# Rotary score products of a latent attention: 128 rows with zeros in place of 64 rows

## The chip, the cores and the metric

The kernel runs on one core of a Trainium2 chip. The metric is the device time of one execution in microseconds (us), lower is better. The engines are named as in the profile: PE (TensorE, the matrix engine; PEld is its weight load), DVE (VectorE), ACT (ScalarE), POOL (GpSimd) and SP (SyncE, which here issues DMA transfers).

## What is computed

One layer of an encoder for two groups of 256 tokens (512 tokens in all), 1024 features, float32: a token mixer with two branches (retention, and an attention over compressed latents), a merge, and a gated convolution with a down projection. What the change touches is the score of the attention's 8 heads:

```python
def _mla_attention(q_nope, q_rope, k_nope, k_rope, v):
    ...
        s = jnp.einsum('bqhd,bkhd->bhqk', qn, k_nope) + jnp.einsum('bqhr,bkr->bhqk', qr, k_rope)
        p = jax.nn.softmax(s.astype(jnp.float32) * scale, axis=-1).astype(v.dtype)
        return jnp.einsum('bhqk,bkhe->bqhe', p, v)
```

A head's query and key have 128 features without position (nope) and 64 rotary ones (rope). The rotary key is one for all heads.

## The kernel before, in words

PE multiplies in a rounded 32-bit format (fp32r), so each float32 matrix is held as two exact parts, high and low (`_h` and `_l`; `split` makes them with a cast on ACT and a subtraction on DVE), and a product is three: high by high, high by low, low by high (`mm3`, lines 157 to 159).

**The rotary part of the scores.** For the rotary key there are two tiles of 128 partitions by 512 tokens, filled at lines 670 to 677 from one transposed bank (`ps_kr`): `K2` holds the high part twice, in partitions 0 to 63 and again in 64 to 127, and `KL` holds the low part twice in the same way. For a head's rotary query, `mla_proj` fills a tile `q2` of 128 partitions: for even heads (parity `i` = 0) the high part lies in partitions 0 to 63 and the low part in 64 to 127, for odd heads the other way round. So the product of `q2` with `K2` over all 128 partitions (line 754) gives high by high and low by high in one go. The third product, high query by low key (line 755), is taken over the 64 partitions that hold the query's high part, the slice `hp`.

`scores(h, g)` handles one head and one group of 256 tokens (a unit): for each of two query tiles of 128 it issues five products of 256 columns to a half of a PSUM bank (three of `mm3`, line 754, line 755). DVE then takes the maximum of each row (line 757), ACT the exponentials (line 761), and DVE scales by the inverse sums. There are 16 units, so line 755 is issued 32 times.

**The order.** PE's order in this part is written by hand: `mla()` issues the scores of unit n, steps of the next heads' projections (`mla_proj`: `ps_qn`, `ps_kn`, `ps_qr`, `ps_v`), the transposes of unit n - 2 (`flip`, line 775, four of 128 columns to `ps_pt`) and the weighting of unit n - 4 (`weigh`, `ps_av`). `interleave` puts products of the two branches' gates (`ps_gb`, `ps_ga`) between them. The other engines' orders are made by a scheduler when the program is built. The weights of `mla_proj` (`wm`) and of the gates (`wgb`, `wga`) arrive by DMA as raw tiles and are split on ACT and DVE beside the scores.

**Tiles.** `t512` takes a tile of 128 partitions by 512 columns from a pool of 69, which come round as they are let go; `K2` and `KL` are held until the last scores.

```python
                mm3(o, cut(qn, slice(None), qc), cut(kn, slice(None), kc), True, False)
                pe.matmul(o, q2[:, qc], K2[:, kc], start=False, stop=False)
                pe.matmul(o, q2[hp, qc], KL[hp, kc], start=False, stop=True)
```

Of the kernel before, what the change touches and what calls it, by code (L numbers as in the profile page):

```python
# [18 lines left out]
# share of other products between those of the attention, and of the last head of the retention  # L19
FILL_MLA, FILL_RET = 0.46, 7.0  # L20
# chunks of the retention branch's gate that are computed with the attention
EARLY_GA = 1
# rows of w_down, in tiles, whose products are done token tile by token tile at the end
TAIL = 12
# products that keep TensorE's clock up while it waits for the first inputs
# [21 lines left out]
def _const_table():  # L47
    """Tables that depend on the shapes alone: identity, rotary tables, decay exponents."""
    f = np.float32
    cols = {}  # L50

    def angles(dim):
        inv = (f(1.0) / (f(10000.0) ** (np.arange(0, dim, 2, dtype=f) / f(dim)))).astype(f)
        return (np.arange(S, dtype=f)[:, None] * inv[None, :]).astype(f)

    cols["ident"] = np.eye(128, dtype=f)
    ar = angles(128)
    cos, sin = np.cos(ar).astype(f).T, np.sin(ar).astype(f).T
    scale = f(128.0 ** -0.5)
    cols["cosq"] = np.concatenate([cos, cos], 0)  # L60
    cols["sinq"] = np.concatenate([-sin, sin], 0)
    cols["cosk"] = cols["cosq"] * scale
    cols["sink"] = cols["sinq"] * scale
    am = angles(64)
    cm, sm = np.cos(am).astype(f), np.sin(am).astype(f)
    cols["cosm"] = np.concatenate([cm.T, cm.T] * 2, 0)
    cols["sinm"] = np.concatenate([-sm.T, sm.T] * 2, 0)
    two = lambda a: a.reshape(2, 128, 64).transpose(1, 0, 2).reshape(128, 128)
    cols["cost"] = two(np.concatenate([cm, cm], 1))
    cols["sint"] = two(np.concatenate([-sm, sm], 1))  # L70
    p = np.arange(128)[:, None]
    j = (p // 64 * 16 + p % 16) * 16 + np.arange(16)[None, :]
    cols["expo"] = -np.abs(j - 255).astype(f)
    at, where = 0, {}
    for k, v in cols.items():
        where[k] = (at, at + v.shape[1])
        at += v.shape[1]
    return np.ascontiguousarray(np.concatenate(list(cols.values()), 1).astype(f)), where
# [11 lines left out]
def interleave(main, filler, ratio):  # L90
    """Runs main; after each step, filler for ratio times main's cost so far. Then the rest of filler."""
    spent, done = 0.0, 0.0
    alive = True
    for cost in main:
        spent += cost
        while alive and done < ratio * spent:
            try:
                done += next(filler)
            except StopIteration:
                alive = False  # L100
    drain(filler)
# [8 lines left out]
def encoder_kernel(ctx: ExitStack, tc: tile.TileContext, ins, outs):  # L110
# [96 lines left out]
    def k_cols(w, k0, k, c0, f, name, step=1024):  # L207
        """Rows k0*128.. of w (as p k f), f columns from c0."""
        h, l = w_chunk(lambda raw: [(kf(raw, k, f), w[:, k0:k0 + k, c0:c0 + f])], k * f, name, step)
        return kf(h, k, f), kf(l, k, f)  # L210

    # first loads, in the order of their use: x and the first shift and scale, then the latents' weights
# [7 lines left out]
    def load_ada(q, k):  # L220
        """256 columns of the shift and of the scale, rows k * 128.."""
        raw = ada_raw[q, k] = t512(F32, f"wada{q}_{k}")
        src = w_ada[:, k, :].rearrange("p (s f) -> p s f", f=D)[:, 0:2, q * 256:(q + 1) * 256]
        nc.sync.dma_start(halves(raw), src)
# [25 lines left out]
    # vectors by rows, turned to features on partitions later  # L250
# [30 lines left out]
    def keep_warm(n):  # L281
        """Products that nothing reads: TensorE's clock is full only while it is busy."""
        for _ in range(n):
            pe.matmul(warm, ones, wide, start=True, stop=True)
# [14 lines left out]
    def rstd_of(var, eps, n, name):  # L299
        """(var + eps) ** -0.5 for [128, n]."""  # L300
        ve, rs = small(n, name + "_ve"), small(n, name + "_rs")
        dve.tensor_scalar(out=halves(ve) if len(var.shape) == 3 else ve, in0=var, scalar1=eps, scalar2=None, op0=ALU.add)
        pool.tensor_tensor(out=rs, in0=ve, in1=half_m[:, :n], op=ALU.pow)
        return rs

    def ln_mv(parts, name):
        """Mean and variance, and rstd, of rows that lie in parts of equal length."""
        st = spool.tile([128, 12], F32, tag="st", name=name + "_st", bufs=6)
        for i, part in enumerate(parts):
            dve.bn_stats(out=st[:, 6 * i:6 * i + 6], in_=part)  # L310
        mv = small(2, name + "_mv")
        dve.bn_aggr(out=mv, in_=st[:, :6 * len(parts)])
        return mv, rstd_of(mv[:, 1:2], LN_EPS, 1, name)
# [7 lines left out]
    def norm_x():  # L321
        """Layernorm of x, rows of tokens, in place."""
# [17 lines left out]
    # vectors with features on partitions  # L340
# [17 lines left out]
    def ada_sums(q, ks=range(NK)):  # L358
        """Four rows of weights at a time, each to its own 32 columns of the array and partitions of the bank."""
        if ks[0] == 0:  # L360
            ps_ada[q] = ps512(f"ps_ada{q}")
        for k in ks:
            o = 32 * (k % 4)
            pe.matmul(ps_ada[q][o:o + 32, :], c32[:, k, :], ada_raw.pop((q, k)), start=(k < 4), stop=(k >= 4))
# [7 lines left out]
    def ada_done(q):  # L372
        """Rows to features on partitions, the sum of the four parts, the biases."""
# [13 lines left out]
    def modulated(ps_of, sc, sh, k, groups, dst, name, on_act, between=None):  # L387
        """dst = parts of ps * sc + sh for feature tile k."""
# [54 lines left out]
    dscr = dpool.tile([128, 16], F32, name="dscr")  # L443

    def decay_start():
        """Powers of sigmoid(decay), as (1 + e ** -decay) ** -distance."""
# [11 lines left out]
    def decay_tile(h):  # L458
        """Decay of key k (row) towards query 255 - m (column m)."""
        d = t512(F32, f"decay{h}")  # L460
        for kt in range(2):
            src = bass.AP(dscr.tensor, dscr.offset + h * 512 + kt * 128, [[1, 128], [1, 256]])
            nc.gpsimd.dma_start(d[:, kt * 256:(kt + 1) * 256], src)
        return d

# [5 lines left out]
    def ada_chunk(which, cc):  # L471
        """512 columns of one adaptive parameter: a generator of its steps."""
# [38 lines left out]
    # ================= start: latents of the attention =================  # L511
    with tc.manual_schedule(engines={PE}):
# [4 lines left out]
        # gate of the attention branch: kept before its sigmoid  # L517
# [33 lines left out]
        # gate of the retention branch: its first chunks are kept before the sigmoid  # L551
# [84 lines left out]
        # latents: root mean square norms, rotary key, then features on partitions  # L636
# [33 lines left out]
        K2, KL = t512(F32R, "K2"), t512(F32R, "KL")  # L670
# [5 lines left out]
        sub(KL[0:64], ps[0:64], as32(K2[0:64]))  # L676
        act.copy(KL[64:128], as32(KL[0:64]))
        take(fill_b, 2.6)

        # ================= latent attention =================  # L680
# [6 lines left out]
        def rope(ps, cos, sin, block, name):  # L687
            """Rotates the halves of each block of partitions."""
# [56 lines left out]
        def scores(h, g):  # L745
# [3 lines left out]
            hp = slice(64 * i, 64 * i + 64)  # L749
            for qt in range(2):  # L750
# [4 lines left out]
                pe.matmul(o, q2[hp, qc], KL[hp, kc], start=False, stop=True)  # L755
# [70 lines left out]
        # ================= the branch's output =================  # L826
# [16 lines left out]
        # ================= retention =================  # L843
# [109 lines left out]
        # a step of the later parameters now and then  # L953
# [15 lines left out]
        # ================= merge =================  # L969
# [32 lines left out]
        # ================= first residual and norms =================  # L1002
# [10 lines left out]
        def residual(ps, xr, gate, name):  # L1013
            """alpha * x + gate * ps, in place of x."""
# [54 lines left out]
        # ================= gated convolution =================  # L1069
# [4 lines left out]
        def up_weights(f, small_tiles=False):  # L1074
            """Parts of the weights of feature tile f: functions of (k, which half)."""
# [51 lines left out]
        # ================= down projection, second residual and norm =================  # L1127
# [6 lines left out]
        def down_w(c, k0, n, small_tiles=False):  # L1134
            """Parts of n rows of weights: a function of (row, first column, last column)."""
# [7 lines left out]
        def finish(t, c, a, b, ps):  # L1143
            """Columns a..b of half c of token tile t: residual and its sums."""
# [8 lines left out]
        for c in range(2):  # L1153
# [3 lines left out]
            # (token tile, first column, last column, bank); the last piece is small  # L1157
# [66 lines left out]
```

## Time and profile before

| what | value |
|---|---|
| time, median of 3 runs | 895.59 us (895.43 to 895.75) |
| profiled execution, first to last instruction (its span) | 893.5 us |
| profiled execution, its own device time | not shown apart from the span; the runs' median is 2.1 us above the span |
| PE busy | 877.2 us, 98% of the span, 4485 products |
| PEld busy | 736.5 us, 82% |
| DVE busy | 570.4 us, 64% |
| ACT busy | 354.3 us, 40% |
| POOL busy | 49.8 us, 6% |
| mean granted clock of PE | 0.994 of full speed |

How to read it: products on PE are pipelined, and the profile models their ends, so a product's duration is longer than the time that it takes from the next one. The start of each is recorded, and the distance from one start to the next (called a step here) tells what a product costs the sequence.

### The profile page before, as it was taken

To read this page: it belongs to the slowest core of one execution; us is meant where nothing else is said; L and a number is where in the kernel's file an instruction comes from. 1 tells how busy PE (TensorE), PEld (TensorE's weight loads), DVE (VectorE), ACT (ScalarE), POOL (GpSimd) and SP (SyncE) were. 2 spreads that over 40 slices of the span, in tenths; PEclk is the share of its full clock that TensorE was granted. 3 is DMA by queue.
4 is the path that set the end of the run, shared out by engine and by line. 5 is a ranking of instruction groups with operands and counts; after the bars stand their busy time and mean duration, and the time that the engine had idled before them with its cause. 6 is when DMAs were issued, how large, how long until landed. Compare 5 with 4: busy or idle time off the path is not lost.

```text
span 893.5 us, 11463 instructions
## 1 busy us (share of the span) xinstructions
PE 877.2 (98%) x4485; PEld 736.5 (82%) x4485; DVE 570.4 (64%) x950; ACT 354.3 (40%) x585; POOL 49.8 (6%) x78
## 2 busy tenths in 40 slices
PE   8999999999999999999998999999999999999996
PEld 5778788888889898988886899888888888888885
DVE  5475877684677777885974966447755755323456
ACT  3555766562343443353342166333333343212200
POOL 3030000000000001000020200000000000100001
PEclk9999999999999999999998999999999999999999
DMA  9922212233545425344356323234334533622401
GB/s 302 388 83 60 70 57 92 67 123 95 153 142 182 113 95 153 131 169 161 111 185 206 111 95 94 60 106 153 119 100 137 160 102 122 208 81 93 142 23 71
DMA packets 118374, 114.29 MB, mean 128 GB/s; under 512 B 6853, under 2 KB 97187, under 8 KB 118320
## 3 DMA queue, kind: packets, MB, share of 16 engines
q1 hardware_dynamic: 114688, 104.00, 35.4%
q0 software_dynamic: 2912, 8.45, 3.3%
q10 hardware_dynamic: 720, 1.11, 0.3%
q8 instruction: 35, 0.57, 0.3%
q14 instruction: 19, 0.16, 0.0%
HBM read 109.34 MB, written 4.20 MB: 127 GB/s over the span
## 4 chain that ended last, share of the span: by engine, by line
PE 94%; DMA 2%; DVE 1%; ACT 1%; issue 0%; SPq 0%; DVEq 0%; ACTq 0%
PE ps_b L157 5%; PE ps_d L157 5%; PE ps_b L159 5%; PE ps_d L159 5%; PE ps_b L158 5%; PE ps_d L158 4%; PE ps_a L158 4%; PE ps_a L159 4%; PE ps_a L157 4%; PE ps_rv L159 2%; PE ps_rv L158 2%; PE ps_rv L157 2%; PE ps_gb L157 2%; PE ps_ga L157 2%; PE ps_ga L159 2%; PE ps_ga L158 2%
## 5 line engine op out<-in xcount | busy, mean ns | idle before, releaser
L484 DVE SCALAR_TENSOR_TENSOR acc<-araw,csil,acc 128x512 f32<-128x512 f32 x112 | 78.3, 746 | 8.1 <-DMA araw<-in_w_ada_dram 8.1
L157 PE MATMUL ps_b<-h_h,wup_h 128*128 128x512 f32 (+1 forms) x200 | 72.9, 364 | 0.3 <-ACT h2m L394 0.3
L158 PE MATMUL ps_a<-h_l,wup_h 128*128 128x512 f32 (+1 forms) x200 | 73.0, 365 | 0.1
L157 PE MATMUL ps_a<-h_h,wup_h 128*128 128x512 f32 (+1 forms) x200 | 72.8, 364 | 0.0
L159 PE MATMUL ps_b<-h_h,wup_l 128*128 128x512 f32 (+1 forms) x200 | 72.8, 364 | 0.0
L158 PE MATMUL ps_b<-h_l,wup_h 128*128 128x512 f32 (+1 forms) x200 | 72.8, 364 | 0.0
L159 PE MATMUL ps_a<-h_h,wup_l 128*128 128x512 f32 (+1 forms) x200 | 72.8, 364 | 0.0
L158 PE MATMUL ps_d<-wd_l,g_h 128*128 128x512 f32 (+1 forms) x198 | 72.5, 366 | 0.0
L157 PE MATMUL ps_d<-wd_h,g_h 128*128 128x512 f32 (+1 forms) x198 | 72.5, 366 | 0.0
L159 PE MATMUL ps_d<-wd_h,g_l 128*128 128x512 f32 (+1 forms) x198 | 72.4, 366 | 0.0
L148 ACT CAST wup_h<-wup_r 128x1024 fp32r<-128x1024 f32 (+1 forms) x46 | 44.3, 1013 | 49.7 <-PE ps_b L158 36.7
L139 DVE TENSOR_TENSOR wd_l<-wd_r,wd_h 128x1024 fp32r<-128x1024 f32 (+1 forms) x24 | 26.2, 1132 | 58.6 <-ACT wd_h L148 58.4
L139 DVE TENSOR_TENSOR wup_l<-wup_r,wup_h 128x1024 fp32r<-128x1024 f32 (+1 forms) x46 | 52.2, 1174 | 11.3 <-ACT wup_h L148 9.5
L148 ACT CAST wd_h<-wd_r 128x1024 fp32r<-128x1024 f32 (+1 forms) x24 | 22.2, 979 | 73.4 <-PE ps_d L159 69.1
L142 DVE TENSOR_TENSOR conv<-conv,ps_b 128x512 f32<-128x512 f32 x22 | 15.1, 687 | 56.7 <-PE ps_b L159 53.6
L157 PEld LDWEIGHTS ps_b<-h_h,wup_h 128*128 128x128 f32 x200 | 37.8, 189 | 6.4 <-ACT h2m L394 0.5
L158 PEld LDWEIGHTS ps_a<-h_l,wup_h 128*128 128x128 f32 x200 | 37.8, 189 | 6.3 <-DVE h_l L139 0.3
L158 PEld LDWEIGHTS ps_b<-h_l,wup_h 128*128 128x128 f32 x200 | 37.7, 189 | 5.9
L157 PEld LDWEIGHTS ps_a<-h_h,wup_h 128*128 128x128 f32 x200 | 37.7, 189 | 5.9
L159 PEld LDWEIGHTS ps_a<-h_h,wup_l 128*128 128x128 f32 x200 | 37.8, 189 | 5.9
L159 PEld LDWEIGHTS ps_b<-h_h,wup_l 128*128 128x128 f32 x200 | 37.8, 189 | 5.9
L158 PEld LDWEIGHTS ps_d<-wd_l,g_h 128*128 128x128 f32 x198 | 37.4, 189 | 6.1
(329 smaller groups left out, 2261.0 us busy)
## 6 DMA issues: line engine op xcount, KB each, us to landing
wup_r<-in_w_up_dram SPq DMA_DIRECT2D x44, 512.0 KB, 4.7
araw<-in_w_ada_dram SPq DMA_DIRECT2D x64, 256.0 KB, 5.4
wd_r<-in_w_down_dram SPq DMA_DIRECT2D x10, 1024.0 KB, 4.8
wada<-in_w_ada_dram SPq DMA_DIRECT2D x32, 256.0 KB, 6.0
wga_r<-in_w_in_dram SPq DMA_DIRECT2D x4, 1024.0 KB, 5.0
wmo_r<-in_w_mla_o_dram SPq DMA_DIRECT2D x4, 1024.0 KB, 4.6
wqk_r<-in_w_in_dram SPq DMA_DIRECT2D x8, 512.0 KB, 4.2
wrv_r<-in_w_in_dram SPq DMA_DIRECT2D x4, 1024.0 KB, 5.5
```

Of the source, the lines that this page charges most:

```text
L139: (eng or dve).tensor_tensor(out=out, in0=a, in1=b, op=ALU.subtract)
L142: (eng or dve).tensor_tensor(out=out, in0=a, in1=b, op=ALU.mult)
L148: act.copy(hi, src)
L157: pe.matmul(out, l[0], r[0], start=start, stop=False)
L158: pe.matmul(out, l[0], r[1], start=False, stop=False)
L159: pe.matmul(out, l[1], r[0], start=False, stop=stop)
L484: dve.scalar_tensor_tensor(out=acc[g], in0=raw, scalar=s, in1=acc[g], op0=ALU.mult, op1=ALU.add)
```

## The change

The keys' low part lies in two tiles in place of one, one for each parity of the head. Each has the low part in the 64 partitions that face the query's high part, and zeros in the other 64, written once by POOL. The third product then runs over all 128 partitions; the query's low part meets the zeros. The sum is the same.

```diff
-        K2, KL = t512(F32R, "K2"), t512(F32R, "KL")
+        K2 = t512(F32R, "K2")
+
+        KL = [t512(F32R, f"KL{i}") for i in range(2)]
+        for i in range(2):
+            pool.memset(as32(KL[i][64 - 64 * i:128 - 64 * i]), 0.0)
         ps = ps512("ps_kr")
...
         act.copy(K2[64:128], ps[0:64])
-        sub(KL[0:64], ps[0:64], as32(K2[0:64]))
-        act.copy(KL[64:128], as32(KL[0:64]))
+        sub(KL[0][0:64], ps[0:64], as32(K2[0:64]))
+        act.copy(KL[1][64:128], as32(KL[0][0:64]))
...
             kc = slice(g * 256, g * 256 + 256)
-            hp = slice(64 * i, 64 * i + 64)
             for qt in range(2):
...
                 pe.matmul(o, q2[:, qc], K2[:, kc], start=False, stop=False)
-                pe.matmul(o, q2[hp, qc], KL[hp, kc], start=False, stop=True)
+                pe.matmul(o, q2[:, qc], KL[i][:, kc], start=False, stop=True)
```

Comments and docstrings are left out in the changed file as well, which moves no instruction. Lines behind the edit move: the two rotary products stand at 757 and 758 then, and the memsets at 674.

On PE the order of all products stays. The place is the first unit's first query tile; `ps_s` is the bank of scores, numbers are those of buffers. Before:

```order
L754 MATMUL ps_s_0_1032<-K_885,q2a_973 128x256 [waits DVE_49]
L755 MATMUL ps_s_0_1032<-KL,q2a_973 128x256
L157 MATMUL ps_s_0_1032<-kn_0_h,qn_0_h 128x256
L158 MATMUL ps_s_0_1032<-kn_0_l,qn_0_h 128x256
L159 MATMUL ps_s_0_1032<-kn_0_h,qn_0_l 128x256
```

And with the change:

```order
L757 MATMUL ps_s_0_1035<-K_885,q2a_976 128x256 [waits DVE_49]
L758 MATMUL ps_s_0_1035<-KL_886,q2a_976 128x256 [waits Pool_49]
L157 MATMUL ps_s_0_1035<-kn_0_h,qn_0_h 128x256
L158 MATMUL ps_s_0_1035<-kn_0_l,qn_0_h 128x256
L159 MATMUL ps_s_0_1035<-kn_0_h,qn_0_l 128x256
```

The first product with each of the two KL tiles now waits for POOL; the other 30 wait for nothing new. On POOL the two memsets stand between the last inverse root of the latents' norms (`rms_rs`) and the loads of the retention's decay:

```order
 L303 TENSOR_TENSOR rms_rs<-rms_ve,half_m 128x2 [waits DVE_49] x3
 L303 TENSOR_TENSOR rms_rs<-rms_ve,half_m 128x2 [waits DVE_49,Pool_49]
-L463 DMA decay_2709<-dscr 128x256 [waits DMASW1_49,DMASW7_49,DMASW0_49,DMAHW4_49,DVE_49,PE_49]
-L463 DMA decay_2709<-dscr 128x256 [waits DMASW2_49]
+L674 MEMSET KL_886 64x512 [waits PE_49,Pool_49]
+L674 MEMSET KL_887 64x512 [waits DMAHW4_49,PE_49]
+L463 DMA decay_2712<-dscr 128x256 [waits DMASW1_49,DMASW0_49,DMASW7_49,DVE_49,PE_49]
+L463 DMA decay_2712<-dscr 128x256 [waits DMASW2_49]
```

The memsets wait for the last readers of the tiles that they take over, and nothing else is put ahead of them. The orders of DVE, ACT and SP stay.

## Rows read from the trace of the kernel before

**Rows 1.** The page: busy time of each engine (share of the span) and count of instructions; and the chain of work that ended last, by engine.

```profile
PE 877.2 (98%) x4485; PEld 736.5 (82%) x4485; DVE 570.4 (64%) x950; ACT 354.3 (40%) x585; POOL 49.8 (6%) x78
PE 94%; DMA 2%; DVE 1%; ACT 1%; issue 0%; SPq 0%; DVEq 0%; ACTq 0%
```

**Rows 2.** Busy time by stretches, of the whole stage of the scores and of 15 us within it. Columns: stretch, its length, busy us (instructions) of PE, PEld, DVE, ACT and POOL, granted clock of PE as a share of full speed, busy share of the DMA engines, GB/s.

```profile
88.00:178.00 90.00, 90.00 (x496) 73.69 (x496) 67.80 (x130) 59.22 (x137) 0.00 (x0) 1.00 0.22 70
148.00:163.00 15.00, 15.00 (x89) 12.62 (x88) 14.03 (x24) 12.36 (x27) 0.00 (x0) 1.00 0.32 112
```

**Rows 3.** Who waited for whom, on PE, from 73 to 185 us: us in total, times, longest.

```profile
PE ps_qn L158 <- DVE cqT_l L139: 0.5, 1, 0.5
```

**Rows 4.** Timeline of PE around the end of the first unit and the first products behind it. Columns: start us, duration us, engine, line, operation, out<-in, rows x columns of the array, partitions x columns of the output.

```profile
88.73 0.38 PE L755 MATMUL ps_s<-KL,q2a 64*128 64x256 f32 x1
89.04 0.39 PE L157 MATMUL ps_s<-kn_h,qn_h 128*128 128x256 f32 x1
89.26 0.28 PE L158 MATMUL ps_s<-kn_l,qn_h 128*128 128x256 f32 x1
89.38 0.28 PE L159 MATMUL ps_s<-kn_h,qn_l 128*128 128x256 f32 x1
89.50 0.28 PE L754 MATMUL ps_s<-K,q2a 128*128 128x256 f32 x1
89.71 0.38 PE L755 MATMUL ps_s<-KL,q2a 64*128 64x256 f32 x1
90.02 0.50 PE L157 MATMUL ps_qn<-cqT_h,wm_h 128*128 128x512 f32 x1
90.59 0.49 PE L159 MATMUL ps_qn<-cqT_h,wm_l 128*128 128x512 f32 x1
```

**Rows 5.** Timeline of the weight loads (PEld) for the same products; columns as before.

```profile
89.38 0.19 PEld L754 LDWEIGHTS ps_s<-K,q2a 128*128 128x128 f32 x1
89.70 0.18 PEld L755 LDWEIGHTS ps_s<-KL,q2a 64*128 64x128 f32 x1
90.02 0.19 PEld L157 LDWEIGHTS ps_qn<-cqT_h,wm_h 128*128 128x128 f32 x1
```

**Rows 6.** All products that read the tile KL: count, duration ns (least, median, most), first and last start us.

```profile
L755 PE MATMUL ps_s<-KL,q2a x16: 378/380/382, 88.7 to 169.3; 64*128 64x256 f32 x16
L755 PE MATMUL ps_s<-KL,q2b x16: 379/382/382, 103.1 to 176.9; 64*128 64x256 f32 x16
```

**Rows 7.** Timeline of PE around the last of these products.

```profile
176.72 0.28 PE L754 MATMUL ps_s<-K,q2b 128*128 128x256 f32 x1
176.93 0.38 PE L755 MATMUL ps_s<-KL,q2b 64*128 64x256 f32 x1
177.25 0.66 PE L775 MATMUL ps_pt<-cst,p 128*128 128x128 f32 x4
177.66 0.48 PE L157 MATMUL ps_ga<-h_h,wga_h 128*128 128x512 f32 x1
```

**Rows 8.** Timeline of PE, three pieces: the start of a unit; a product on 64 rows followed by products of 512 columns; and four transposes with no product on 64 rows before them.

```profile
95.02 0.28 PE L157 MATMUL ps_s<-kn_h,qn_h 128*128 128x256 f32 x1
95.13 0.28 PE L158 MATMUL ps_s<-kn_l,qn_h 128*128 128x256 f32 x1
...
96.56 0.38 PE L755 MATMUL ps_s<-KL,q2a 64*128 64x256 f32 x1
96.87 0.50 PE L157 MATMUL ps_gb<-h_h,wgb_h 128*128 128x512 f32 x1
97.20 0.39 PE L158 MATMUL ps_gb<-h_l,wgb_h 128*128 128x512 f32 x1
97.44 0.40 PE L159 MATMUL ps_gb<-h_h,wgb_l 128*128 128x512 f32 x1
...
108.97 0.60 PE L775 MATMUL ps_pt<-cst,p 128*128 128x128 f32 x4
109.33 0.36 PE L157 MATMUL ps_s<-kn_h,qn_h 128*128 128x256 f32 x1
```

**Rows 9.** Timeline of DVE behind the first scores: the low part of the second pair's projection weights, with no idle time before it.

```profile
89.71 0.81 DVE L139 TENSOR_TENSOR wm_l<-wm_r,wm_h 128x640 fp32r<-128x640 f32 x1
```

**Rows 10.** Timelines of ACT, DVE and PE around the first chunk of the retention's gate; in brackets the idle time of the engine before the row, and what ended it.

```profile
148.32 2.01 ACT L148 CAST wga_h<-wga_r 128x1024 fp32r<-128x1024 f32 x2 [1.49 <-PE ps_gb L158]
...
146.97 0.69 DVE L757 TENSOR_REDUCE nm<-ps_s 128x2 f32<-128x512 f32 x1 [3.78 <-PE ps_s L755]
149.50 2.35 DVE L139 TENSOR_TENSOR wga_l<-wga_r,wga_h 128x1024 fp32r<-128x1024 f32 x2
...
151.32 0.39 PE L159 MATMUL ps_ga<-h_h,wga_l 128*128 128x512 f32 x1
```

**Rows 11.** Timelines of POOL (a constant of one column, two powers) and of DVE (its largest memset, and its first work behind the latents' norms); brackets as before.

```profile
0.24 0.10 POOL L1212 MEMSET const-float32-0.0<- 128x1 f32 x1 [0.24 <-issue]
44.19 3.26 POOL L453 TENSOR_TENSOR dtab<-dbase,cst 128x16 f32<-128x16 f32 x1 [29.62 <-DMA cst<-in_cst_dram]
64.37 0.70 POOL L303 TENSOR_TENSOR rms_rs<-rms_ve,half_m 128x2 f32<-128x2 f32 x1 [2.05 <-DVE rms_ve L302]
...
0.99 0.27 DVE L276 MEMSET c<- 128x256 f32 x1
72.43 0.75 DVE L665 TENSOR_SCALAR cqT_f<-ps_lt,vecs 128x512 f32<-128x512 f32 x1 [4.82 <-PE ps_lt L663]
```

## The prediction

> **What bounds the kernel now.** The page comes first: TensorE (PE) is busy for 98% of the span and makes 94% of the chain that ended last [rows 1]. So only what shortens PE's own sequence, or what PE waits for, can move the time. The change touches the attention's scores, which run from about 88 to 178 us; the table by stretches shows PE busy for all 90.00 of those 90 us, at a granted clock of 1.00 (the 2.4 GHz level), with VectorE (DVE) at 67.80 and ScalarE (ACT) at 59.22 [rows 2]. The view of PE's waits finds one wait of 0.5 us between 73 and 185 us, and that one lies in the projections ahead of the scores [rows 3]. A stage like this ends when PE has issued its list, so the figure to read is not the duration of a product (neighbours overlap) but the step from one product's start to the next one's start.
>
> Read that way, the timeline of PE shows something that busy time hides [rows 4]. Inside one chain of 128x256 products the step is 0.12 us (89.26, 89.38, 89.50). Around the product that the change edits (L755, on 64 rows) it is not: 0.21 from the rotary product with K2 (L754) to it, 0.31 from it to the next product, and 0.22 for that next one, which is again an ordinary 128-row product. The weight loads tell how this comes about [rows 5]: the load of L754 starts at 89.38, one step ahead of its product at 89.50, but the load of L755 starts at 89.70 with its product at 89.71, and the load behind it starts at 90.02 with its product at 90.02. Where 64 rows follow 128, or 128 follow 64, the load isn't hidden behind the product before.
>
> The view of the tile KL has 32 such products, 16 per parity of the head, first at 88.7 and last at 176.9 us, with median durations within 2 ns of each other [rows 6]. The last one shows the same steps as the first ones, 0.21 and then 0.32 [rows 7].
>
> **The change part by part.** *The 64-row product becomes a 128-row one.* No product is added or removed, and PE's order stays. The price of one is the excess of three steps over those of an unbroken chain:
> - followed by a 256-column product: 0.21 + 0.31 + 0.22 against 3 x 0.12, so 0.38 us;
> - followed by a 512-column product, as at 96.56: 0.21 + 0.31 + 0.33 against 0.12 + 0.12 + 0.23 (the last from 97.20 to 97.44, rounded), so 0.38 us [rows 8];
> - followed by the four transposes of a flip: from their start to the next product 0.41 us at 177.25 [rows 7] against 0.36 at 108.97, where no 64-row product stands before them [rows 8]. That is 0.05 in place of 0.10, so 0.33 us.
>
> In the program's order five of the 32 are followed by transposes; so 32 x 0.38 - 5 x 0.05 = 11.9 us. After the change these products and their neighbours all have 128 rows, and I take the ordinary step of 0.12 for each: L754 streams the same 256 columns into the same bank, with the same stationary tile, already. Bounds: no step falls (0 us), or all fall to 0.11 (95.02 to 95.13 [rows 8]), 96 x 0.01 = 1.0 us more.
>
> Here a page has another view. The Trainium skill, "TensorE: Matmul & The Clock Gate", section "LDWEIGHTS (loading the stationary operand)", says that a weight load's time goes with its columns and that the number of rows doesn't matter. By that alone 64 or 128 rows cost the same, and the sum would be 0 us, 895.6. The trace agrees on the load itself, 0.18 against 0.19 us [rows 5], but the steps differ by far more than the loads do; what is lost is the overlap, and I go by the steps.
>
> *What the shorter list runs into.* The first unit (88.73 to 90.02) gains nothing: the third product of ps_qn, at 90.59, waits for wm_l, which DVE ends at 89.71 + 0.81 = 90.52, behind work that doesn't wait for PE [rows 9]. So two of the 32 are lost, 0.77 us, and 11.1 us remain. The next near miss is the split of the first gate chunk: wga_l, two halves on DVE from 149.50 to 151.85, the first (ended by about 150.7) read by PE at 151.32 [rows 10]. If it stayed where it is, PE would lose there all it had gained. But ACT's cast before it waited 1.49 us for PE (ps_gb), and DVE's row before stood idle 3.78 us for PE's scores [rows 10]: both move forward with PE. In a dense stretch, 148 to 163, DVE works 14.03 us of 15 [rows 2]; four 64-row products start in it, so PE would need 15 - 4 x 0.38 = 13.5, and DVE would be 0.5 longer. I charge nothing, since the program flips a unit two units after its scores and weighs it four units after, and over the stage DVE's 67.80 us fit well into what is left of 90; if that cover failed it would cost 0.5 us.
>
> *Two memsets on POOL, 64x512 each, and a wait of PE for each, once.* They stand behind the last rms_rs, which ends at 64.37 + 0.70 = 65.07 [rows 11], and what stands behind them on POOL is a load for the retention, which comes after the attention. KL for even heads is read first at 88.73, for odd heads at 103.1 [rows 6], so the cover is 23.6 us for one and 38 us for both. No row shows a POOL memset of this size. From below: 0.10 us (a constant of one column). From above: POOL's own slope on its slowest kind of work, (3.26 - 0.70) / 14 columns = 0.18 us a column between the 128x2 and the 128x16 power, so 94 us. DVE's memset of 128x256 took 0.27 [rows 11], which is the nearest in kind; I take some 0.5 to 3 us each, all covered. If they slow DVE beside them, DVE stands idle for 4.82 us before 72.43 anyway [rows 11].
>
> *One more buffer held.* KL takes two of the 69 tiles in place of one, until the scores end; some later transfers and casts wait for other tiles. They gain or lose tenths at most while PE has the work of a unit in hand; I take 0. *The copy and subtraction that fill KL* keep size and engine: 0.
>
> **Sum.** 893.5 - 11.1 = 882.4 us of span. The three runs lie at 895.43 to 895.75, 2.1 above the profiled span; the profile tells no other time of that execution, so 2.1 is what I add: **884.5 us**. Nothing behind 178 us can give the time back unless PE meets a wait there; the page has PE at 98% over the whole span.
>
> **The rivals.**
> 1. *A wait takes over half of it.* If wga_l or its like doesn't move with PE, the 18 products before 151 us that gain keep only the 0.6 us between the end of its first half and its use, and the 12 after it give 12 x 0.38 - 4 x 0.05 = 4.4: 5.0 us in all, 890.6. Against it speaks that the casts before it wait for PE [rows 10]. Chance 0.07. A milder form, in which each of the four later weight splits that this stage's products read (wm2, wgb3, wm3, wga0) eats two products as the first wm_l does, takes 4 x 0.77 = 3.1 us, and with the 0.5 us of DVE's dense stretch 3.6: 888.1; that is still the forecast's case.
> 2. *Nothing changes.* The overlap may be lost for another reason than the 64 rows, say because K2 and KL follow each other with the same stationary tile q2; then the steps stay, and the time with them, at 895.6. Against it: the first two products of mm3 share their stationary tile too, and step by 0.11 at 95.02 [rows 8]. The Trainium skill, same page, section "The mechanism", says that a weight load overlaps a running product only when the row group differs; by that rule a 128-row product with KL would not be loaded ahead either, and the time would stay at 895.6. The trace contradicts it: the load at 89.38 starts while L159 runs on the same 128 rows [rows 4, 5]. Chance 0.06.
> 3. *Slower: POOL's memset comes late.* PE takes its list in order, so it would stand at 88.73 until the zeros are there. It decides from 23.6 us for the first memset, or 38 us for both. At the upper bound of 94 us each the second ends at 65.1 + 188 = 253, PE stands some 150 us longer before the odd heads' first score, and the time is about 1034; just past the point it is 884.5 plus the lateness, slower than before once that is over 11.1 us. Chance 0.04, since a memset is not a power.
>
> **How the numbers follow.** The forecast has 0.83, and it is the likeliest. Its own range goes from 882.5 (no loss in the first unit, 0.77, and steps of 0.11, 1.0: 882.7, with 0.2 for the scatter of the runs) to 888.1 (that milder form). The three rivals together hold 0.17, so the range needs no more than this: 882.5 to 888.1. About 0.2%, 1.8 us, is what a measurement of this kernel tells from no change; forecast and first rival are both faster by more, 0.83 + 0.07 = 0.90; same 0.06; slower 0.04.
>
> **What would show it.** In the changed kernel's timeline the product with KL must have 128 rows and steps of 0.12 before and behind it, its weight load one step ahead; the next product must step by 0.12 or 0.23. The scores' stage should end near 167 us in place of 178, with PE still busy for all of it and DVE near 68 us of some 79. PE's waits should show wm_l at about 90 us with under 1 us, and none for POOL. If the steps stay at 0.21 and 0.31, rival 2 holds; if PE waits for DVE near 150 us by several us, rival 1; if it waits for POOL, rival 3.

## The result and the profile after

The change took 884.11 us (median of 4 runs, 883.79 to 884.81) against 895.67 us before (895.43 to 896.64): a ratio of 0.9869, 95% interval [0.9855, 0.9883], 11.6 us less. The prediction was 884.5, with a range of 882.5 to 888.1. The profiled span fell from 893.5 to 883.0 us, by 10.5; where the other 1.1 us lies is told below.

The page of the kernel after, busy time of the engines:

```profile
PE 864.1 (98%) x4485; PEld 732.1 (83%) x4485; DVE 569.5 (64%) x950; ACT 354.4 (40%) x585; POOL 50.4 (6%) x80
```

PE issues the same 4485 products and is busy 13.1 us less (10.5 us of span, and 2.6 us that it now stands idle in longer waits, of which more below); the other engines do what they did [rows 1]. The timeline of PE shows where, in the piece that answers to [rows 4]:

```profile
88.28 0.28 PE L157 MATMUL ps_s<-kn_h,qn_h 128*128 128x256 f32 x1
...
88.64 0.33 PE L757 MATMUL ps_s<-K,q2a 128*128 128x256 f32 x1
88.80 0.28 PE L758 MATMUL ps_s<-KL,q2a 128*128 128x256 f32 x1
88.92 0.28 PE L157 MATMUL ps_s<-kn_h,qn_h 128*128 128x256 f32 x1
89.03 0.28 PE L158 MATMUL ps_s<-kn_l,qn_h 128*128 128x256 f32 x1
89.15 0.28 PE L159 MATMUL ps_s<-kn_h,qn_l 128*128 128x256 f32 x1
89.27 0.28 PE L757 MATMUL ps_s<-K,q2a 128*128 128x256 f32 x1
89.39 0.28 PE L758 MATMUL ps_s<-KL,q2a 128*128 128x256 f32 x1
89.86 0.50 PE L157 MATMUL ps_qn<-cqT_h,wm_h 128*128 128x512 f32 x1 [0.19 <-ACT wm_h L148]
90.20 0.40 PE L158 MATMUL ps_qn<-cqT_l,wm_h 128*128 128x512 f32 x1
90.75 0.50 PE L159 MATMUL ps_qn<-cqT_h,wm_l 128*128 128x512 f32 x1 [0.15 <-DVE wm_l L139]
```

The reader is to subtract starts. From 88.80 to 89.39, across both products with KL (L758), every step is 0.12 us (one reads 0.11), where 0.21, 0.31 and 0.22 stood. So it is at the other products with KL too: 0.12 ahead of each of them from the second on. The unit's last product starts at 89.39 in place of 89.71, though the scores began 0.21 later, and then the bottom rows show what eats that: PE stands for wm_h and wm_l, and the third product of ps_qn starts at 90.75, in place of 90.59. The weight loads of the same stretch, against [rows 5], are now a step ahead of their products; the one with KL starts at 89.27, its product at 89.39:

```profile
89.15 0.19 PEld L757 LDWEIGHTS ps_s<-K,q2a 128*128 128x128 f32 x1
89.27 0.19 PEld L758 LDWEIGHTS ps_s<-KL,q2a 128*128 128x128 f32 x1
```

At the end of the stage, against [rows 7]:

```profile
165.95 0.28 PE L757 MATMUL ps_s<-K,q2b 128*128 128x256 f32 x1
166.07 0.28 PE L758 MATMUL ps_s<-KL,q2b 128*128 128x256 f32 x1
166.19 0.60 PE L778 MATMUL ps_pt<-cst,p 128*128 128x128 f32 x4
166.55 0.49 PE L157 MATMUL ps_ga<-h_h,wga_h 128*128 128x512 f32 x1
```

The steps are 0.12, and the four transposes take 0.36 from start to next start, as they do elsewhere. All products that read KL, and the memsets that made its zeros (count, duration ns, first and last start us):

```profile
L758 PE MATMUL ps_s<-KL,q2a x16: 279/283/283, 88.8 to 160.0; 128*128 128x256 f32 x16
L758 PE MATMUL ps_s<-KL,q2b x16: 282/283/285, 102.4 to 166.1; 128*128 128x256 f32 x16
L674 POOL MEMSET KL<- x2: 519/521/523, 65.3 to 65.9; 64x512 f32 x2
```

The stage by its own clock: before, from the first product of the scores to the first transpose behind the last one, 177.25 - 88.07 = 89.18 us; after, 166.19 - 88.28 = 77.91. That is **11.27 us less, against 11.1 forecast**. The start in the kernel before is this row of its timeline:

```profile
88.07 0.28 PE L157 MATMUL ps_s<-kn_h,qn_h 128*128 128x256 f32 x1
```

PE's waits from 73 to 185 us, against [rows 3]: us in total, times, longest. POOL isn't among them.

```profile
PE ps_qn L158 <- DVE cqT_l L139: 0.5, 1, 0.5
PE ps_qn L157 <- ACT wm_h L148: 0.2, 1, 0.2
PE ps_qn L159 <- DVE wm_l L139: 0.2, 1, 0.2
```

And busy time over the stage, with the columns of [rows 2]: in 80 us DVE does what it did in 90, and PE is short of full by the first unit's wait alone.

```profile
88.00:168.00 80.00, 79.66 (x502) 71.22 (x501) 67.42 (x130) 60.24 (x141) 0.00 (x0) 1.00 0.25 79
```

**Where the other 1.1 us is.** The 11.6 compares medians and the 10.5 two single executions; the profiled one of the kernel after was the slowest of its four (884.81 us, 0.7 above their median). Against the 11.27 of the stage it began its scores 0.21 us later, and behind them it lost 0.56 (883.0 - 166.19 against 893.5 - 177.25). That loss has one place, the output projection (`ps_f`, 208 products), some 300 us behind the change: from its first product to its last it took 52.30 us before and 52.95 after; all PE starts between the scores and there moved by the same amount. PE's longest wait there, in the kernel before, after, and in a second profile of the kernel after:

```profile
PE ps_f L157 <- ACT wo_h L148: 3.0, 1, 3.0
```

```profile
PE ps_f L157 <- ACT wo_h L148: 4.5, 1, 4.5
```

```profile
PE ps_f L157 <- ACT wo_h L148: 4.1, 1, 4.1
```

The same program shows 4.5 and 4.1, and experiments below show 3.1 to 4.3 with either kind of product. So the wait is older than the change and its length goes with the execution, not with the row count. Of the 1.5 us by which it is longer here, 0.8 came back right behind it: before, 12 steps in a row behind the wait were 0.43 us or more, in place of the 0.23 of a product of 512 columns at full clock; after, 8 were.

### The profile page after: what moved, and what is told of

Its sections match the earlier page's. It is cut to its first block, busy times and chain, and to the rows that moved or that the text cites. A ratio compares the mean times of both kernels' runs of the same rounds, so it can differ in the third digit from the quotient of the medians.

```text
span 883.0 us, 11470 instructions
## 1 busy us (share of the span) xinstructions
PE 864.1 (98%) x4485; PEld 732.1 (83%) x4485; DVE 569.5 (64%) x950; ACT 354.4 (40%) x585; POOL 50.4 (6%) x80
## 4 chain that ended last, share of the span: by engine, by line
PE 92%; DVE 2%; DMA 2%; ACT 2%; issue 0%; SPq 0%; DVEq 0%; ACTq 0%
PE ps_b L157 5%; PE ps_d L157 5%; PE ps_b L159 5%; PE ps_d L159 5%; PE ps_d L158 5%; PE ps_b L158 5%; PE ps_a L158 5%; PE ps_a L159 4%; PE ps_a L157 4%; PE ps_rv L159 2%; PE ps_rv L158 2%; PE ps_rv L157 2%; PE ps_ga L157 2%; PE ps_ga L158 2%; PE ps_rqk L157 2%; PE ps_ga L159 2%
## 5 line engine op out<-in xcount | busy, mean ns | idle before, releaser
L139 DVE TENSOR_TENSOR wup_l<-wup_r,wup_h 128x1024 fp32r<-128x1024 f32 (+1 forms) x46 | 52.2, 1173 | 13.4 <-ACT wup_h L148 11.6
```

Source lines behind the costliest of these rows:

```text
L139: (eng or dve).tensor_tensor(out=out, in0=a, in1=b, op=ALU.subtract)
```

## Experiments

Two theories and what would tell them apart. **The change of row count**: where a product on 64 rows follows one on 128, or the other way round, PE loses the hiding of a weight load, a cost per change. **The form**: a product on 64 rows costs its 0.38 us wherever it stands. Beside them, that the gain came from something else which the edit brought (other tiles, other waits, zeros).

### 64 rows again, with the new tiles and zeros

```diff
-                pe.matmul(o, q2[:, qc], KL[i][:, kc], start=False, stop=True)
+                hp = slice(64 * i, 64 * i + 64)
+                pe.matmul(o, q2[hp, qc], KL[i][hp, kc], start=False, stop=True)
```

> The two KL tiles and POOL's zeros as in the change, but the third product again over the 64 partitions that hold the query's high part. Theory (each change between 64 and 128 rows costs PE the hiding of a weight load): the steps are 0.21, 0.31 and 0.22 us as before and the time is that of before, 895.7, within 1 us. Rival (the gain came from the tiles' new places or the moved waits, not from the rows): about 884.

Measured: 895.5 us against 895.58, ratio 0.9998 [0.9988, 1.0008]. The timeline has the old steps back, 0.21 (96.33 to 96.54), 0.31 and 0.34; the last is that of a 512-column product, 0.33 at this place before [rows 8]:

```profile
96.33 0.28 PE L757 MATMUL ps_s<-K,q2a 128*128 128x256 f32 x1
96.54 0.38 PE L759 MATMUL ps_s<-KL,q2a 64*128 64x256 f32 x1
96.85 0.50 PE L157 MATMUL ps_gb<-h_h,wgb_h 128*128 128x512 f32 x1
97.19 0.39 PE L158 MATMUL ps_gb<-h_l,wgb_h 128*128 128x512 f32 x1
```

The gain hangs on the rows of the product; the second tile, the memsets and the moved waits are worth nothing that shows either way (0.1 us, with an interval of about 1 us to each side).

### 128 rows for even heads alone

```diff
-                pe.matmul(o, q2[:, qc], KL[i][:, kc], start=False, stop=True)
+                hp = slice(64, 128) if i else slice(0, 128)
+                pe.matmul(o, q2[hp, qc], KL[i][hp, kc], start=False, stop=True)
```

> The change for even heads alone; odd heads keep 64 rows. Theory: 16 of the 32 products gain, 16 x 0.38 - 2 x 0.05 (two are followed by transposes) - 0.77 (first unit, which waits for wm_l anyway) = 5.2 us, so 890.5, and 883 us of span become about 888. If the gain needs all products (an engine state that holds over the stage), it is near 0; if the first change alone brings it, near 11.

Measured: 890.51 us against 895.58, ratio 0.9943 [0.9928, 0.9957]: 5.1 us, with 5.2 expected: half of the products bring a little under half of the gain, as a price per product has it. In the trace the even heads' products with KL have steps of 0.12 and the odd heads' 0.21 and 0.31, side by side. Both forms stand in one profile:

```profile
L759 PE MATMUL ps_s<-KL,q2a x16: 279/283/286, 88.4 to 164.1; 128*128 128x256 f32 x16
L759 PE MATMUL ps_s<-KL,q2b x16: 379/381/381, 102.1 to 171.4; 64*128 64x256 f32 x16
```

### 64 rows as before, but two such products next to each other

```diff
-                mm3(o, cut(qn, slice(None), qc), cut(kn, slice(None), kc), True, False)
-                pe.matmul(o, q2[:, qc], K2[:, kc], start=False, stop=False)
-                pe.matmul(o, q2[hp, qc], KL[hp, kc], start=False, stop=True)
+                if qt == 0:
+                    mm3(o, cut(qn, slice(None), qc), cut(kn, slice(None), kc), True, False)
+                    pe.matmul(o, q2[:, qc], K2[:, kc], start=False, stop=False)
+                    pe.matmul(o, q2[hp, qc], KL[hp, kc], start=False, stop=True)
+                else:
+                    pe.matmul(o, q2[hp, qc], KL[hp, kc], start=True, stop=False)
+                    pe.matmul(o, q2[:, qc], K2[:, kc], start=False, stop=False)
+                    mm3(o, cut(qn, slice(None), qc), cut(kn, slice(None), kc), False, True)
```

> The kernel before, all products over as many rows as before, but the second query tile of a unit takes its third rotary product first and its three others last, so that the two products on 64 rows stand next to each other. Theory (the cost is that of a change of row count): 0.21 into the pair, 0.12 inside it, 0.31 and 0.22 behind it; one change in and out per unit in place of two, 16 x 0.38 - 5 x 0.05 - 0.38 (first unit) = 5.4 us less, 890.3. Rival (a product on 64 rows costs its 0.38 wherever it stands, since its weights are never loaded ahead): the step inside the pair is about 0.3 and the time stays within 1.6 us of before, 894 to 895.7.

Measured: 890.2 us against 895.58, ratio 0.9939 [0.9924, 0.9954]: 5.4 us, as expected of the change of row count, and out of reach of the form. The steps lie a little otherwise than expected. PE's timeline:

```profile
94.99 0.28 PE L159 MATMUL ps_s<-kn_h,qn_l 128*128 128x256 f32 x1
95.11 0.28 PE L755 MATMUL ps_s<-K,q2a 128*128 128x256 f32 x1
95.32 0.38 PE L756 MATMUL ps_s<-KL,q2a 64*128 64x256 f32 x1
95.54 0.28 PE L758 MATMUL ps_s<-KL,q2a 64*128 64x256 f32 x1
95.75 0.38 PE L759 MATMUL ps_s<-K,q2a 128*128 128x256 f32 x1
95.97 0.28 PE L157 MATMUL ps_s<-kn_h,qn_h 128*128 128x256 f32 x1
96.09 0.28 PE L158 MATMUL ps_s<-kn_l,qn_h 128*128 128x256 f32 x1
```

And its weight loads:

```profile
95.32 0.18 PEld L756 LDWEIGHTS ps_s<-KL,q2a 64*128 64x128 f32 x1
95.42 0.19 PEld L758 LDWEIGHTS ps_s<-KL,q2a 64*128 64x128 f32 x1
95.75 0.19 PEld L759 LDWEIGHTS ps_s<-K,q2a 128*128 128x128 f32 x1
95.85 0.19 PEld L157 LDWEIGHTS ps_s<-kn_h,qn_h 128*128 128x128 f32 x1
```

The load of the second product on 64 rows starts 0.12 ahead of its product (95.42, 95.54): such loads are hidden like any other, if 64 rows ran before. Only the first load behind a change starts with its product (95.32; 95.75). The four steps are 0.21, 0.22, 0.21, 0.22. So one change lengthens two steps of 0.12, that ahead of it by 0.09 and that behind it by 0.10, **0.19 us** together; the 16 pairs agree within 0.01, but for the step into the first one (0.29). In the kernel before, the way in and the way out lay on neighbouring products, and the middle step of 0.31 held a part of both. The two products of a pair use the same 64 rows; no run has products on different halves next to each other, so whether that is a change too stays open.

### The low part in both halves, no zeros

```diff
-        K2 = t512(F32R, "K2")
-
-        KL = [t512(F32R, f"KL{i}") for i in range(2)]
-        for i in range(2):
-            pool.memset(as32(KL[i][64 - 64 * i:128 - 64 * i]), 0.0)
+        K2, KL = t512(F32R, "K2"), t512(F32R, "KL")
...
-        sub(KL[0][0:64], ps[0:64], as32(K2[0:64]))
-        act.copy(KL[1][64:128], as32(KL[0][0:64]))
+        sub(KL[0:64], ps[0:64], as32(K2[0:64]))
+        act.copy(KL[64:128], as32(KL[0:64]))
...
-                pe.matmul(o, q2[:, qc], KL[i][:, kc], start=False, stop=True)
+                pe.matmul(o, q2[:, qc], KL[:, kc], start=False, stop=True)
```

> 128 rows, but one KL tile with the low part in both halves as in the kernel before, and no zeros: the query's low part then meets the key's low part, so the fourth product (low by low) is added to the score. Theory: what counts is the row count, so 884.1 as with the change, within 1 us, steps of 0.12; the memsets, at 0.52 us each and over 20 us ahead of their reader, were free. Rival (zeros or the second tile matter): away from 884 by more than 1.5 us.

Measured: 884.47 us against 895.58, ratio 0.9871 [0.9857, 0.9886], the change's time, with the steps of 0.12:

```profile
L754 PE MATMUL ps_s<-KL,q2a x16: 274/283/283, 88.6 to 159.8; 128*128 128x256 f32 x16
```

The zeros buy no time: the tile of the kernel before was already fit for a product over 128 rows, which then adds low by low, a term that the exact product of both parts contains. This is the change with one tile and two memsets less.

### The wait that was there before

```diff
+                hi, lo = t512(F32R, name + "_h"), t512(F32R, name + "_l")
+                last_wo[:] = [act.copy(hi, raw[:, k * 512:(k + 1) * 512])]
...
+                    r = act.copy(hi[:, a:a + 1024], raw[:, a:a + 1024])
+                    if f == 0:
+                        tc.add_manual_dep(r.ins, last_wo[0].ins.name, ...)
```

(Cut to the lines that matter. The first two are in load_wo, the others in up_weights: on ACT the casts of wup0 stand behind the last cast of wo.)

> The change, and beside it one order on ACT: the casts of the first up-projection weights (wup0) stand behind the last four casts of w_out (wo) in place of between them. In every profile so far PE waited 3.0 to 4.5 us for those casts (ps_f for wo_h, behind a wup_h cast that waits for its transfer), before the change (3.0) and after (4.5), and that difference is most of why the profiled span fell by 10.5 and the runs' median by 11.6. Theory (the wait is ACT's order, not the change's doing, and its length varies with the transfers): the wait goes, 884.1 less 3.5 to 5.0, so 879 to 881. Rival (w_out itself arrives late, or another wait takes its place): 883 to 885.

> The change itself once more, unedited, on the same chip: 884.1 within 0.7 us; a second profile, whose wait of ps_f for wo_h tells how far that wait varies between executions of one program: by the profiles so far anywhere between 3.0 and 4.5 us, with the span moving along.

Measured on one chip: the change again 883.93 us (one run of the four at 886.42), ratio 0.9875 [0.9858, 0.9891]; with the order on ACT **876.87 us**, ratio 0.9787 [0.9772, 0.9801] against 895.75, the fastest of all. That is 7.1 us below the change, over the 3.5 to 5.0 expected and outside the 879 to 881. The wait is gone and none took its place. ACT's timeline in that kernel: the four casts of wo run at 456.64, and only then ACT waits 6.11 us for the transfer.

```profile
456.64 2.18 ACT L984 CAST wo_h<-wo_r 128x512 fp32r<-128x512 f32 x4
464.93 2.00 ACT L1092 CAST wup_h<-wup_r 128x1024 fp32r<-128x1024 f32 x2 [6.11 <-DMA wup_r<-in_w_up_dram]
```

In the kernel after, ACT waited for the same transfer with those casts behind it:

```profile
465.95 1.04 ACT L148 CAST wup_h<-wup_r 128x1024 fp32r<-128x1024 f32 x1 [8.92 <-DMA wup_r<-in_w_up_dram]
466.90 0.61 ACT L148 CAST wo_h<-wo_r 128x512 fp32r<-128x512 f32 x1
```

The first expectation also put most of the difference between 10.5 and 11.6 down to this wait; by the lengths of the output projection above it made 0.65 us of it. What it missed in the price is PE's clock. Stretches of the kernel after, with the columns of [rows 2]:

```profile
460.00:465.00 5.00, 3.09 (x14) 2.23 (x12) 0.00 (x0) 0.00 (x0) 0.00 (x0) 1.00 0.73 276
465.00:470.00 5.00, 1.88 (x4) 1.12 (x4) 2.97 (x4) 4.05 (x6) 0.00 (x0) 0.59 0.01 2
470.00:475.00 5.00, 4.91 (x17) 3.58 (x16) 3.09 (x5) 0.02 (x1) 0.00 (x0) 0.73 0.76 225
471.00:472.00 1.00, 1.00 (x3) 0.81 (x3) 1.00 (x3) 0.00 (x0) 0.00 (x0) 0.50 0.46 118
```

And of the kernel with the order on ACT:

```profile
460.00:465.00 5.00, 5.00 (x24) 4.15 (x23) 0.69 (x1) 0.07 (x1) 0.00 (x0) 1.00 1.07 360
465.00:470.00 5.00, 5.00 (x24) 4.15 (x23) 3.95 (x4) 3.94 (x4) 0.00 (x0) 1.00 0.23 69
```

With the wait, the granted clock averages 0.59 and 0.73 of full in the ten us that hold its end and the products behind it. From 466 to 472, by stretches of 1 us, it is 0.50, the 1.2 GHz level: it fell while PE stood idle, and products of 512 columns then start 0.43 us apart (471.24, 471.67, 472.09) in place of 0.23. Without the wait the clock stays at 1.00.

All of the 7 us lies there. From its first product to its last the output projection took 52.38 us in the second profile of the change and 45.06 with the order on ACT, 7.3 less; from 40 us to there PE's starts in the two differ by 0.1 us at most. The waits that the profile lists for PE are 4.6 of it (4.1 for wo_h and 0.5 for wo_l). The other 2.7 are the products at the lower clock and a second, short wait for wo_l, which shows on PE's weight loads alone. In the kernel after that is this load:

```profile
470.65 0.29 PEld L158 LDWEIGHTS ps_f<-wo_l,mg_h 128*128 128x128 f32 x1 [0.81 <-DVE wo_l L139]
```

## Why the prediction was right

**The steps as the price.** 0.38 us per product was read from the starts of a few products in the trace before and taken for all 32, and it held: half the products gave 5.1 of 5.2 us, halving the changes gave 5.4 of 5.4. The products' busy time would have misled, at 0.38 against 0.28 a difference of 0.10, or 3.2 us for 32: it leaves out the step ahead of the product and the longer step of the one behind it. That a weight load takes the same time for 64 rows (0.18 us) and 128 (0.19) was true and beside the point. So the rule of the Trainium skill, "TensorE: Matmul & The Clock Gate", section "LDWEIGHTS (loading the stationary operand)", by which only the columns count, holds for the load and told nothing of the time.

**What the prediction took for the cause.** It spoke of a load that isn't hidden where the row count changes; the pair of products shows just that, and sizes it at 0.19 us per change. The Trainium skill, "TensorEngine Tiling (Array Packing)", section "Key Properties", says that a change of tiling mode drains TensorE. The trace fits that, with 0.09 us lost ahead of a change and 0.10 behind it; that the loss is such a drain no run here shows.

**The first unit.** Forecast: no gain, 0.77 us lost to wm_l. Seen: the third product of ps_qn at 90.75 against 90.59, and the whole run started its scores 0.21 later; so a gain of 0.05. Beside wm_l, the prediction's one wait, PE stood 0.19 for wm_h, which it had not named.

**What was charged nothing, and cost nothing.** The split of the gate's first chunk moved forward with PE: wga_l ran from 143.01, and PE showed no wait there. DVE's dense stretch cost nothing; over the stage PE waited only in the first unit. The memsets took 0.52 us each, at DVE's pace (0.27 for half as many columns), and were over by 66.4, 22 us ahead of their reader. The chunk's low part, on DVE after the change:

```profile
143.01 2.35 DVE L139 TENSOR_TENSOR wga_l<-wga_r,wga_h 128x1024 fp32r<-128x1024 f32 x2
```

**The sum.** 11.1 forecast; 11.27 in the stage by the profile, 11.6 and 11.8 by the medians of the two measurements. The forecast is a little low in the stage, by 0.2; the rest lies within the intervals of the measurements, about 1.3 us to each side, and one source of scatter is known, the wait for wo_h. The 2.1 us that the prediction added to the span are the median less the span of a faster execution: wherever a run's time and span are both known, they differ by 1.7 to 1.8. That moves nothing, since the forecast is the median before less the 11.1. The prediction said that nothing behind 178 us could give the time back unless PE met a wait there, and took PE's 98% for an answer. The 98% hid a wait of 3.0 us with a slow clock behind it. It did not fail the forecast, since it is there with either kernel at about the same price; with the change in, taking it away was worth 7.1 us, over half of what the change itself brought.

**The rivals.** That a wait takes half of it, and that the memset is late, are refuted by PE's waits above; that nothing changes, by the time; that something other than the rows did it (K2 and KL in turn with the same q2, or the tiles and waits that the edit brought), by the steps after the change and by the first experiment.

## What to carry to other kernels

Price a product by the distance to the next one's start, and look at the steps on either side of it; a product on fewer rows can cost its neighbours more than itself. Where rows change back and forth inside a dense chain, fill them up (with zeros, or with a part whose product belongs to the sum anyway, as here the low part's copy) or put the short ones next to each other; each change avoided gave 0.19 us here. And go through PE's waits one by one over the whole span, however full it looks: one wait of 4 us was worth 7.

## What the runs showed of the hardware that was not expected

- A change of row count (64 to 128 or back, products of 256 columns, granted clock 1.00) costs PE 0.19 us, in both directions alike, split into 0.09 before and 0.10 behind it; between two products on the same 64 rows the load is hidden, 0.12 us ahead of its product.
- A wait of 4.5 us in the middle of a full list ended at a granted clock of 0.50, which held for some 5 us of products behind it; taking the wait away (4.1 us long in the profile of the run compared) gave 7.1 us.
